# Seven products for eight in part of the input projection, with attention laid among the plain gate tiles

## The chip, the core and the metric

The kernel runs on one core of a Trainium2 chip. TensorE (PE) multiplies, VectorE (DVE) and ScalarE (ACT) work elementwise, GpSimd (POOL) and SyncE (SP) mostly issue transfers. The metric is the device time of one execution, in microseconds.

## The reference, cut to what matters

One layer of a streaming encoder on 1088 frames: 1024 of a new stream and 64 of a running one with a key and value cache.

```python
def mixer(xn, conv_prefix, attn_fn, w_in, w_conv, w_conv_out, w_attn_out, w_out):
    proj = xn @ w_in                      # 1024 -> 5120
    cb, cc, ch, q, k, v, ga, gb = jnp.split(proj, splits, axis=-1)   # 6 x 512, 2 x 1024
    cv, conv_state = causal_conv(cc * ch, conv_prefix, w_conv)
    ya = (cb * cv) @ w_conv_out
    o, new_k, new_v = attn_fn(heads(q), heads(k), heads(v))
    yb = o.reshape(B, L, ATT_DIM) @ w_attn_out
    merged = jax.nn.sigmoid(ga) * ya + jax.nn.sigmoid(gb) * yb
    return merged @ w_out, conv_state, new_k, new_v

x = x + mixer(rmsnorm(x, g_mix), ...)
x = x + swiglu(rmsnorm(x, g_ffn), w_ff1, w_ff3, w_ff2)      # 1024 -> 2816 -> 1024
return rmsnorm(x, g_final), ...           # and the rolled caches and convolution states
```

Attention has 8 heads of 64. Each chunk of 64 frames reads itself and the 8 chunks before it, with a bias by relative distance.

## The kernel before, in words

All matrix work is done in pairs of rounded numbers: `split` writes a high part (ScalarE, line 129) and the rest as a low part (VectorE, line 130), and a product is three matmuls, high by high, high by low and low by high (`product`, lines 182 to 184, weights of 128 columns stationary, frames moving).

The stages follow each other:

- **Head** (lines 354 to 455). For each of nine token tiles: `norm_tile` takes the sum of squares and the factor, transposes the tile on TensorE and copies it; `scale_tile` transposes the factor, scales by it and the gain, and splits into `xn`; `v_tile` makes the value columns (lines 423 to 425, 24 matmuls of 512 columns). `cache_tile` (line 456) turns the cached keys; keys, queries and values go to DRAM in the layout of heads.
- **Projection tiles**, 128 output columns each. `run_dense` makes one tile in three pieces of frames, `CH`: 384, 384 and 320, eight row blocks by three matmuls each, 72 matmuls. Order: q and k in turn (8 tiles), gate a (8), gate b (8). Gates go to DRAM (`ga_d`, `gb_d`).
- **Attention**, as a generator of 75 steps. A step makes the scores of one query tile (lines 570, 571), adds the bias (533), takes the exponential (543) and scales (545); it transposes an earlier step's tile (600) and splits it into `pt`; and it multiplies a still earlier one with the values (625) and adds halves (552 to 554). After each piece of the tiles from the fourth on, `between` runs `PER` = 1.16 steps. Scores and their transposes share the two buffers of `patt`.
- **Convolution**: 12 tiles cc, ch, cb by `dense` in the same pieces; in between, the attention output is read back from `o_d` and split into `ob` (line 757).
- **Merge**: `ya` and `yb`, 16 tiles of 36 matmuls, with the gates read back, sigmoid applied, and the sum split into `mg` (as quarters of 512 rows by 544 frames) and `ms`.
- **Output projection** (lines 843 to 848), norm and transposes (917), with `first_half` and `second_half` making the seven operands of the hidden layer (line 942 the differences).
- **Hidden layer**: `Unit` and `run` make two tiles at once in seven products of quarter matrices for eight (Strassen's way in Winograd's form): seven steps of 24 matmuls of 272 columns (line 1047), with sums of weights prepared a step at a time while the unit before runs, and results added from PSUM and snapshots.
- **Down projection** (line 1385), also by seven products, final norm and output.

The order of instructions on each engine is not simply that of the text. A planner with its own estimate of each instruction's duration goes through the program at compile time and gives each engine the first instruction, in text order, that it expects to be ready; pool buffers are handed out in the same pass. At run time each engine keeps the order it was given and waits on semaphores. SP and POOL issue the transfers, each in its own order.

Of the kernel before, what the change touches and what calls it, by code (L numbers as in the profile page):

```python
# [30 lines left out]
CH = [(0, 384), (384, 384), (768, 320)]  # L31
NC = len(CH)
# [6 lines left out]
AHEAD = 1  # L39
PER = 1.16  # L40


def spots(a, n):


    edges = [(0, 512, 0), (512, 1024, 544)]
    r = []
    for lo, hi, at in edges:
        s, e = max(a, lo), min(a + n, hi)
        if s < e:  # L50
            r.append((s - a, at + s - lo, e - s))
    return r


class Acts:


    def __init__(self, tiles):
        self.t = tiles

    def at(self, l, k, o, n):
        return self.t[k // 4][:, l, k % 4, o : o + n]

    def four(self, g, l, o, n):
        return self.t[g][:, l, :, o : o + n]


class Quarters:

# [4 lines left out]
    def at(self, l, k, o, n):  # L74
        h = o // HT
        return self.t[k // 4, h][:, l, k % 4, o - h * HT : o - h * HT + n]


@with_exitstack
def encoder_kernel(ctx: ExitStack, tc: tile.TileContext, ins, outs):  # L80
# [10 lines left out]
    a_stack = ExitStack()  # L91
    apool = a_stack.enter_context(tc.tile_pool(name="apool", bufs=1, reuse_waits="tile", side="right"))
    rpool = ctx.enter_context(tc.tile_pool(name="rpool", bufs=2, reuse_waits="tile"))
    w_stack = ExitStack()
    wpool = w_stack.enter_context(tc.tile_pool(name="wpool", bufs=3, reuse_waits="tile"))
# [7 lines left out]
    g_mix = cols[:, :KD]  # L103
# [4 lines left out]
    hs_d = dr.tile([NF // 2, P, 2, 2 * TS], F32, name="hs_d")  # L108
    q_d = dr.tile([NH, 2, HD, T], F32, name="q_d")
# [5 lines left out]
    bias_e = dr.tile([NH, 768], F32, name="bias_e")  # L115

    def bias_rows(h, a, n):
        return bias_e[h : h + 1, a : a + n].to_broadcast([P, n])
# [8 lines left out]
    def split(hi, lo, src, hi_eng=None):  # L127

        act.copy(hi, src)  # L129
        vec.tensor_tensor(lo, src, hi.bitcast(F32), op=ALU.subtract)  # L130

    def act_tiles(nm):
        return Acts([apool.tile([P, 2, 4, T], F32R, tag=f"A{g}", name=f"{nm}{g}") for g in range(2)])


    units = []
    loads = []

    def plan(view, kt, width, n):

        per = 1 if n == 1 else 2
        for i in range(0, n, per):
            ld = {"src": view[:, i * width : (i + per) * width], "kt": kt, "w": per * width}
            for j in range(per):
# [132 lines left out]
    def q_evac(hp):  # L277
# [7 lines left out]

        return f

    late = []

    def k_out(hp, k32, o, n):  # L290

# [1176 lines left out]
```

## Time and profile before

| | us |
|---|---|
| median of 3 runs (lowest, highest) | 1541.53 (1538.94, 1543.95) |
| the profiled execution | 1541.21 |
| its span, first to last instruction | 1539.3 |
| TensorE busy | 1500.1 |
| weight loads on TensorE busy | 1412.0 |
| VectorE busy | 928.0 |
| ScalarE busy | 623.4 |
| GpSimd busy | 77.5 |
| data moved | 247.18 MB, mean 161 GB/s |

The profile is of one execution. Shares are of the span. A matmul's record includes the time that it spends behind its neighbours, so matmul durations overlap; distances between starts show the rate. Names to the left of an arrow are written, names to the right are read.

### The profile page before, as it was taken

The page shows a single profiled execution, that of the slowest core. Times are in us where ns is not written, and L with a number is a line of the kernel's source. Part 1 is how long each engine was busy: PE and PEld are TensorE (multiplying, and loading weights), DVE is VectorE, ACT ScalarE, POOL GpSimd, SP SyncE. Part 2 cuts the span into 40 slices and gives each one's busy share as a digit, 9 for nine tenths or more (in the row PEclk, how much of TensorE's full clock was granted, in tenths as well). Part 3 has the DMA queues.
Part 4 walks back from the last instruction along what each step waited for, and adds up shares of the span by engine and source line. Part 5 has one row for each costly group of instructions (what it writes and reads, how often), then busy time and mean ns, then how long its engine had stood idle before and what let it go on. Part 6 is the DMA issues. An engine that isn't in the chain of part 4 may idle for free.

```text
span 1539.3 us, 24393 instructions
## 1 busy us (share of the span) xinstructions
PE 1500.1 (97%) x9407; PEld 1412.0 (92%) x9407; DVE 928.0 (60%) x1860; ACT 623.4 (40%) x1236; POOL 77.5 (5%) x146
## 2 busy tenths in 40 slices
PE   7999999999999999999998999999999999899997
PEld 6888999999999999998888999999999999688886
DVE  7524665555553434654379666666666667847677
ACT  7423454444443131543156444444444444502123
POOL 0110000000000000000000010000101111000000
PEclk9999999999999999999999999999999999999999
DMA  8688785444431323545432343333434438777685
GB/s 285 196 239 231 188 251 155 133 139 126 123 103 43 53 75 41 154 146 166 137 126 70 141 144 138 122 118 138 155 141 155 144 138 288 259 240 240 212 266 203
DMA packets 168661, 247.18 MB, mean 161 GB/s; under 512 B 17025, under 2 KB 117265, under 8 KB 168545
## 3 DMA queue, kind: packets, MB, share of 16 engines
q1 hardware_dynamic: 152400, 191.47, 41.1%
q0 software_dynamic: 14992, 52.05, 9.1%
q10 hardware_dynamic: 1152, 2.10, 0.4%
q8 instruction: 74, 1.21, 0.4%
q14 instruction: 43, 0.34, 0.1%
HBM read 161.91 MB, written 85.23 MB: 161 GB/s over the span
## 4 chain that ended last, share of the span: by engine, by line
PE 63%; issue 26%; DMA 4%; POOL 2%; DVE 2%; ACT 1%; SPq 1%; POOLq 0%; ACTq 0%; DVEq 0%
PE A L1385 7%; PE p L182 5%; PE p L183 5%; PE p L184 5%; PE D L1385 3%; PE B L1385 2%; POOL h_d L1105 2%; PE t L600 2%; PE pv L625 2%; PE Ab L1047 2%; DMA w2r<-in_w_ff 1%; PE Aa L1047 1%; PE ys L1242 1%; PE wo L843 1%; PE wo L844 1%
## 5 line engine op out<-in xcount | busy, mean ns | idle before, releaser
L182 PE MATMUL p<-xn,whi 128*128 128x384 f32 (+1 forms) x576 | 192.8, 335 | 0.1
L183 PE MATMUL p<-xn,whi 128*128 128x384 f32 (+1 forms) x576 | 189.2, 328 | 0.0
L184 PE MATMUL p<-xn,wlo 128*128 128x384 f32 (+1 forms) x576 | 189.0, 328 | 0.0
L1385 PE MATMUL A<-ring,ht 128*128 128x512 f32 x528 | 124.9, 390 | 3.9 <-ACT acc L1395 2.2
L1385 PEld LDWEIGHTS A<-ring,ht 128*128 128x128 f32 x528 | 98.7, 188 | 25.9 <-ACT acc L1395 3.5
L182 PEld LDWEIGHTS p<-xn,whi 128*128 128x128 f32 x576 | 109.2, 190 | 1.6 <-DVE kst L130 0.6
L183 PEld LDWEIGHTS p<-xn,whi 128*128 128x128 f32 x576 | 109.3, 190 | 0.1
L184 PEld LDWEIGHTS p<-xn,wlo 128*128 128x128 f32 x576 | 109.0, 189 | 0.0
L533 DVE CUSTOM_DVE_ANT_0 p<-s,bias 128x640 f32<-128x640 f32 (+5 forms) x72 | 47.7, 664 | 97.0 <-PE s L571 96.9
L129 ACT CAST ring<-w2r 128x512 fp32r<-128x512 f32 (+1 forms) x78 | 43.6, 588 | 103.6 <-PE A L1385 51.7
L129 ACT CAST hq<-sa 128x512 fp32r<-128x512 f32 x77 | 47.6, 619 | 89.5 <-DVE sa L1117 55.9
L129 ACT CAST whi<-raw 128x1024 fp32r<-128x1024 f32 x44 | 46.0, 1050 | 92.2 <-PE ch L183 42.5
L130 DVE TENSOR_TENSOR hq<-sa,hq 128x512 fp32r<-128x512 f32 x77 | 53.1, 689 | 37.5 <-ACT hq L129 37.4
L130 DVE TENSOR_TENSOR wlo<-raw,whi 128x1024 fp32r<-128x1024 f32 x44 | 53.7, 1220 | 24.0 <-ACT whi L129 23.9
L1047 PE MATMUL Aa<-tt,wha 128*128 128x272 f32 x352 | 60.9, 295 | 5.2 <-ACT tt L129 3.5
L1385 PE MATMUL D<-ring,ht 128*128 128x512 f32 x264 | 62.9, 390 | 1.4 <-ACT acc L1395 1.4
L130 DVE TENSOR_TENSOR wla<-rawa,wha 128x512 fp32r<-128x512 f32 x56 | 38.4, 687 | 42.3 <-ACT wha L129 42.3
L1105 POOL DMA_DIRECT2D h_d<-hq x77 | 41.0, 533 | 425.0 <-DVE hq L130 248.2
L1385 PEld LDWEIGHTS D<-ring,ht 128*128 128x128 f32 x264 | 49.5, 188 | 12.1 <-ACT acc L1395 1.8
L1047 PE MATMUL Ab<-tt,whb 128*128 128x272 f32 x352 | 58.9, 288 | 1.6 <-ACT whb L129 1.6
L1047 PE MATMUL Ab<-mg,whb 128*128 128x272 f32 x352 | 58.4, 288 | 0.0
L1047 PE MATMUL Aa<-mg,wha 128*128 128x272 f32 x352 | 58.3, 288 | 0.0
(310 smaller groups left out, 3888.1 us busy)
## 6 DMA issues: line engine op xcount, KB each, us to landing
h_d<-hq POOLq DMA_DIRECT2D x77, 512.0 KB, 3.5
ht<-h_d SPq DMA_DIRECT2D x154, 256.0 KB, 3.7
raw<-in_w_in SPq DMA_DIRECT2D x18, 1024.0 KB, 5.9
rawa<-in_w_ff SPq DMA_DIRECT2D x11, 1024.0 KB, 5.7
rawb<-in_w_ff SPq DMA_DIRECT2D x11, 1024.0 KB, 5.3
w2r<-in_w_ff SPq DMA_DIRECT2D x11, 1024.0 KB, 7.2
qd<-q_d SPq DMA_DIRECT2D x32, 272.0 KB, 4.4
x<-in_x_prompt SPq DMA_DIRECT2D x8, 512.0 KB, 4.2
```

What stands on the lines that cost most here:

```text
L129: act.copy(hi, src)
L130: vec.tensor_tensor(lo, src, hi.bitcast(F32), op=ALU.subtract)
L182: mm(out, a, p, start=k == 0, stop=False)
L183: mm(out, a, q, start=False, stop=False)
L184: mm(out, b, p, start=False, stop=k == kt - 1)
L533: vec.tensor_tensor_reduce(out=s if len(ps.shape) == 2 else s.rearrange("p (a b) -> p a b", a=2), in0=ps, in1=bias if len(ps.shape) == 2 e ...
L600: nc.tensor.transpose(tp[:, i * P : (i + 1) * P], s[:, i * P : (i + 1) * P], ident)
L625: mm(pv[:, :, lo:hi], v[:, kb, :], pt[:, :, kb - base, lo:hi], start=i == 0, stop=i == len(blocks) - 1,)
L843: mm(ps, x(k, 0), wh, start=f, stop=False)
L1047: mm(t[:, j, :HN], x[:, k, :], moving(p, l, k, j * HN, HN), start=p in (1, 2, 7) and k == 0 and n == 0, stop=k == 3 and n == 2, skip_group ...
L1105: nc.gpsimd.dma_start(h_d[p, c - 1], hq.rearrange("p i l t -> p (i l t)").bitcast(F32))
L1385: mm(t, ht[k][:, j, x], w[:, l], start=p in (1, 2, 7) and k == 0 and n == 0, stop=k == len(ks) - 1 and n == 2, skip_group_check=p in (6, 5 ...
```

## The change

The normed x is now made and kept as four quarters, like the input of the hidden layer, and the three sums that the seven products need (`xs6`, `xs7`, `xs5`) and a changed fourth quarter are formed in the head, tile by tile (`sums1`), in the order `ORDER` = 8, 0, 1, 4, 2, 5, 3, 6, 7. The scaling by factor and gain is done on rows ahead of the transposes. The plain fourth quarter goes to DRAM (`x21_d`).

Twelve units by seven products follow: q, k, the first four tiles of gate b, and the convolution's cc, ch and cb (two tiles a unit). Their results go to DRAM: q and k to heads, gate b, and the convolution's result `u_d`. The cache tiles are turned during the first two units. Then the plain quarter is read back, and twelve gate tiles (all of gate a, the other half of gate b) are made plainly in four pieces of 272 columns, with attention at `PER` = 2.25 steps a piece; attention ends ahead of the last two tiles (`LAST`), during which u and the attention output are read back. `ya` and `yb` are made in pieces of 272 too. One weight pool, `ws`, serves all stages. `Unit` and `run` are moved up and take operands, banks and snapshots as arguments. Frames are stored by halves of 544 (512 of the prompt, 32 of the sample).

The core of the diff:

```diff
-CH = [(0, 384), (384, 384), (768, 320)]
-NC = len(CH)
...
-AHEAD = 1
-PER = 1.16
...
+PER = 2.25
+LAST = 2
...
+    PIECES = [(j * HN, HN) for j in range(4)]
+    GATES = [("a", m) for m in range(8)] + [("b", m) for m in range(4, 8)]
...
-        for c in cs:
-            o, n = CH[c]
-            ps = pmm.tile([P, 512], F32, tag="mm", name=f"{nm}_{c}")
-            product(ps[:, :n], w, wsl, x, o, n, kt)
...
+    for k in range(KD):
+        nc.tensor.transpose(gp[:, k * P : (k + 1) * P], cols[:, k : k + 1].to_broadcast([P, P]), ident)
+    act.activation(gm, gp, AF.Copy, scale=-0.5)
...
+    def normed(i):
+        n = TT[i][1]
+        xt = xts[i]
+        a = FEW + 6 * (ORDER.index(i) % 2)
+        few = scr[:, a : a + 6]
+        act.activation(scr[:n, SQ : SQ + D], xt[:n], AF.Square, accum_out=few[:n, :1])
+        r = norm_factor(few[:, 1:], few[:n, :1], n, f"m{i}")
+        vec.scalar_tensor_tensor(xt[:n], xt[:n], r[:n], gm[:n], op0=ALU.mult, op1=ALU.mult)
...
+    def left_half(src, c, n):
+        for g in range(2):
+            both(xn.t[g, 0], c, n, src[:, g])
...
+        act.copy(f, src)
+
+    def right_half(src, c, n):
+        for g in range(2):
+            both(xn.t[g, 1], c, n, src[:, g])
+        nc.gpsimd.dma_start(
+            x21_d[:, :, c : c + n],
+            xn.t[0, 1][:, :, :, c : c + n].rearrange("p l k t -> p (l k) t").bitcast(F32),
+        )
...
+        minus(s[:, 0], src[:, 0], f[:, 0])
+        minus(s[:, 1], src[:, 1], s[:, 0])
+        both(t1[6], c, n, s[:, 1])
+        minus(f[:, 0], s[:, 1], f[:, 0])
+        both(t1[7], c, n, f[:, 0])
+        both(t1[5], c, n, s[:, 0])
+        minus(f[:, 1], f[:, 1], s[:, 1])
+        both(xn.t[0, 1], c, n, f[:, 1])
...
+    units = []
+    for nm, u in (
+        ("q", 0), ("q", 1), ("k", 0), ("k", 1), ("gb", 0), ("cc", 0), ("ch", 0), ("cb", 0), ("gb", 1), ("cc", 1),
+        ("ch", 1), ("cb", 1),
+    ):
...
+    turned1(ORDER[0])
+    for n, i in enumerate(ORDER):
+        if n + 1 < len(ORDER):
+            turned1(ORDER[n + 1])
+        if n + 3 < len(ORDER):
+            load_x(ORDER[n + 3])
+        if n + 2 < len(ORDER):
+            normed(ORDER[n + 2])
...
+        v_tile(i)
+        if n == len(ORDER) - 1:
+            for u in (u0, u1):
+                u.prep(0)
+                u.prep(1)
+        sums1(i)
...
+    def summed(src, snap):
+
+        if snap is None:
+            t = snap1(None, None)
+            whole(t, src, None)
+            return t
+        vec.tensor_tensor(snap, src, snap, op=ALU.add)
+        return snap.rearrange("p j n -> p (j n)")
...
+    def q_done(u):
+        def f(r, h, src, snap):
+            s = summed(src, snap)
+            st = stage()
+            act.activation(st[:, 0], s, AF.Copy, scale=0.125)
             vec.scalar_tensor_tensor(
-                st[:, 1, :n], ps, 0.125, st[:, 0, :n].bitcast(F32), op0=ALU.mult, op1=ALU.subtract
+                st[:, 1], s, 0.125, st[:, 0].bitcast(F32), op0=ALU.mult, op1=ALU.subtract
             )
-            to_heads(q_d, st, hp, o, n)
+            to_heads(q_d, st, 2 * u + r, h)
...
+    def k_done(u):
+        def f(r, h, src, snap):
+            kf = slot(CC, HT)
+            whole(kf, src, snap)
+            st = stage()
+            split(st[:, 0], st[:, 1], kf)
+            to_heads(k_d, st, 2 * u + r, h)
+            late.append(lambda: k_out(2 * u + r, h, kf))
...
+    def b_done(u):
+        def f(r, h, src, snap):
+            s = summed(src, snap)
+            nc.sync.dma_start(gb_d[(2 * u + r) * P : (2 * u + r + 1) * P, h * HT : (h + 1) * HT], s)
...
+    def cb_done(u):
+        def f(r, h, src, snap):
+            s = summed(src, snap)
+            for a, at, n in spans(h):
+                vec.tensor_tensor(s[:, a : a + n], s[:, a : a + n], ccs[r][:, at : at + n], op=ALU.mult)
+            st = stage()
+            split(st[:, 0], st[:, 1], s)
+            nc.sync.dma_start(u_d[2 * u + r, :, :, h * HT : (h + 1) * HT], st.bitcast(F32))
...
+    x7 = {p: xn.t[gh] for p, gh in PLAIN.items()} | t1
...
+        for _ in r:
+            if n < 2 and si in (2, 5):
+                i = 2 * n + si // 5
+                cache_tile(i)
+                if i + 2 < 4:
+                    cache_load(i + 2)
+            if si > 1:
+                for f in due:
+                    f()
+                due.clear()
+            due += late
             late.clear()
-            dense(xn, KD, tiles[i], w=w, cs=[c], nm=f"p{i}")
...
+            o, n = PIECES[c]
+            ps = pmm.tile([P, 512], F32, tag="mm", name=f"g{i}_{c}")
+            product(ps[:, :n], gate_w[i], xn, o, n)
+            st = st_pool.tile([P, HN], F32, tag="st", name=f"gst{i}_{c}")
+            act.copy(st[:, :n], ps[:, :n])
+            nc.sync.dma_start(dst[m * P : (m + 1) * P, o : o + n], st[:, :n])
...
-    run_dense(1)
     head_load(0)
+
+    nc.sync.dma_start(xn.t[0, 1].rearrange("p l k t -> p (l k) t").bitcast(F32), x21_d)
     bias_table(2)
-    for i in range(2, len(tiles)):
-        run_dense(i, between if i > 2 else None)
...
+    for i in range(2):
+        gate_w[i] = next_w()
+        gate(i, (0, 1))
+    for i in range(2):
+        for c in (2, 3):
+            gate(i, (c,))
+            if i:
+                between()
+    for i in range(2, len(GATES)):
+        gate_w[i] = next_w()
+        if i == len(GATES) - LAST:
+            for _ in steps:
+                pass
+            att_stack.close()
+            uo = pg_stack.enter_context(tc.tile_pool(name="uo", bufs=1, reuse_waits="tile"))
+            u = Acts(uo.tile([P, 2, 4, T], F32R, name="u"))
+            ob = Acts(uo.tile([P, 2, 4, T], F32R, name="ob"))
+            mp = pg_stack.enter_context(tc.tile_pool(name="mgp", bufs=5, reuse_waits="tile"))
+            for k in range(4):
+                nc.sync.dma_start(u.t[:, :, k].bitcast(F32), u_d[k])
+                t = mp.tile([P, T], F32, tag="ol", name=f"ol{k}", bufs=1)
+                nc.sync.dma_start(t, o_d[k * P : (k + 1) * P])
+                split(ob.t[:, 0, k], ob.t[:, 1, k], t)
+        for c in range(4):
+            gate(i, (c,))
+            between()
...
+    psum2 = pg_stack.enter_context(tc.tile_pool(name="psum2", bufs=5, space=PSUM, reuse_waits="tile"))
+    for m in range(8):
+        wa, wb = next_w(), next_w()
+        sg = {}
+        for o, n in PIECES:
+            for nm, src in (("ga", ga_d), ("gb", gb_d)):
+                t = sg[nm, o] = mp.tile([P, HN], F32, tag=nm, name=f"{nm}{m}_{o}")
+                nc.sync.dma_start(t, src[m * P : (m + 1) * P, o : o + n])
+                act.activation(t, t, AF.Sigmoid)
+            ya = psum2.tile([P, 512], F32, tag="mm", name=f"ya{m}_{o}")
+            product(ya[:, :n], wa, u, o, n)
+            vec.tensor_tensor(sg["ga", o], ya[:, :n], sg["ga", o], op=ALU.mult)
+        for o, n in PIECES:
+            t = sg["ga", o]
+            yb = psum2.tile([P, 512], F32, tag="mm", name=f"yb{m}_{o}")
...
```

More of the change, by code (lines that the diff above doesn't have):

```diff
@@ L271, in to_heads @@
+    def to_heads(dst, st, hp, h):
+        far = 0 if dst is q_d else CACHE
+        for row, at, m in ((512 * h, 0, 512), (TP + far + 32 * h, 512, 32)):
             for j in range(2):
@@ L1255, in up_run @@
         l, p = names[n]
-        return run(unit, (gate_done if l == "a" else hidden_done)(p), ahead)
+        return run(unit, operands, bank2, snap2, (gate_done if l == "a" else hidden_done)(p), ahead)
     u0, u1 = up_unit(0), up_unit(1)
```

970 lines of the change are left out of this document (436 added, 534 removed).

## The prediction

> **What bounds the kernel now.** I read the page first: its engine shares and its row of granted clocks.
>
> ```profile
> span 1539.3 us, 24393 instructions
> PE 1500.1 (97%) x9407; PEld 1412.0 (92%) x9407; DVE 928.0 (60%) x1860; ACT 623.4 (40%) x1236; POOL 77.5 (5%) x146
> PEclk9999999999999999999999999999999999999999
> ```
>
> TensorE is busy 97% of the span at full clock. VectorE has 40% to spare, ScalarE 60%. So columns taken off TensorE should show in the time, as long as the other engines and the transfers keep pace where the work is packed more tightly. Next came the table of busy time by stretch, for the stages that the change rebuilds (columns: stretch, its length, busy us and count for PE, PEld, DVE, ACT, POOL, then clock, DMA share, GB/s).
>
> ```profile
> 0.00:14.00 14.00, 5.82 (x24) 4.79 (x25) 5.90 (x19) 9.47 (x14) 1.39 (x7) 1.00 0.89 335
> 71.50:140.00 68.50, 60.92 (x354) 59.20 (x352) 20.00 (x48) 18.72 (x40) 8.58 (x15) 0.95 0.82 220
> 100.00:110.00 10.00, 6.20 (x29) 5.85 (x28) 4.43 (x8) 3.36 (x6) 2.02 (x3) 0.83 0.80 213
> 120.00:130.00 10.00, 7.39 (x48) 7.20 (x47) 0.81 (x6) 0.25 (x1) 0.00 (x0) 1.00 1.09 303
> 140.00:470.00 330.00, 328.94 (x2084) 319.27 (x2082) 191.27 (x475) 155.64 (x333) 5.28 (x8) 1.00 0.53 154
> 500.00:600.00 100.00, 100.00 (x607) 100.00 (x606) 42.87 (x66) 19.61 (x33) 0.00 (x0) 1.00 0.32 56
> ```
>
> From 140 to 470 us (q, k, gates with attention) and from 500 to 600 us (convolution) TensorE never rests. Between the value products and full attention, 71.5 to 140 us, it loses 7.6 us and some clock. The third view is TensorE in order of time, for its waits.
>
> ```profile
> 14.15 0.78 PE L423 MATMUL pvv<-wvh,xn 128*128 128x512 f32 x1
> 86.83 0.66 PE L456 MATMUL ckp<-ident,ct 128*128 128x128 f32 x4
> 105.11 0.90 PE L295 MATMUL ktp<-ident,k 128*128 128x128 f32 x3 [3.80 <-ACT k L318]
> 129.77 0.44 PE L570 MATMUL s<-kd,qd 128*128 128x384 f32 x1 [2.60 <-DVE mx L533]
> 712.56 0.80 PE L847 MATMUL wo<-woh,ms 128*128 128x512 f32 x1 [2.21 <-ACT woh L129]
> 831.85 0.39 PE L1047 MATMUL Ab<-tt,whb 128*128 128x272 f32 x1 [1.62 <-ACT whb L129]
> 836.92 0.82 PE L1047 MATMUL Aa<-tt,wha 128*128 128x272 f32 x2 [3.47 <-ACT tt L129]
> ```
>
> The four cache transposes at 86.83 run in the middle of the first q tile's products, though the program text has them after it: the order on an engine is the planner's, which puts ready work ahead of work it expects to be late.
>
> **What a column costs.** A busy matmul overlaps its neighbours, so I take distances between starts. Plain tiles go in pieces of 384, 384 and 320 columns, 72 products each. The 100 us from 500 to 600 hold 607 of them, 164.7 ns each, so a plain tile takes 72 x 0.1647 = 11.86 us. The seven-product form is already used for the hidden layer, and the chain of waits shows its steps of 24 products of 272 columns:
>
> ```profile
> 1223.58 3.01 PE Da L1047 x24
> 1226.59 3.01 PE Aa L1047 x24
> ```
>
> That is 125.4 ns a product. A unit of seven steps takes 21.07 us and yields two tiles, which cost 23.72 us plain.
>
> **The change, part by part.**
>
> (1) 24 tiles (four each of q, k and gate b, twelve of convolution) become twelve units: 24 x 11.86 = 284.6 us become 12 x 21.07 = 252.8. That is **-31.8 us** on TensorE, the bound.
>
> (2) The twelve other gate tiles and the sixteen ya/yb products go from three pieces to four of 272 columns. A gate tile has 96 products, 12.04 us: 12 x 0.18 = +2.2. A ya or yb has 48, 6.02 for 5.93: 16 x 0.09 = +1.4. **+3.6**.
>
> The Trainium skill ("TensorE: Matmul & The Clock Gate", section "Wait — 56ns, not 53.3ns?") gives a warm product columns / 2.4 GHz plus about 2.5 ns, which is 116 ns for 272 columns where this trace has 125. By that page part 1 would still be about -32 and part 2 an estimated +1.2 instead of +3.6; the measured pitch decides.
>
> (3) The head. The norm factor now scales whole rows, and nine small transposes of it go; eight transposes for the gain row come, and 24 key transposes for 20. About 0. The first value product waits for the gain row. Its columns come by the POOL queue in 5.6 us:
>
> ```profile
> cols<-in_cols POOLq DMA_DIRECT2D x1, 10.0 KB, 5.6
> ```
>
> With issue, eight transposes, a copy and a scaling I reach about 13 to 14 us, as now (14.15): **0**, ends -2 and +3. The seven operands cost VectorE eight more half-size instructions for each of four token tiles. The same work stands ahead of the hidden layer, and there
>
> ```profile
> 810.00:820.00 10.00, 10.00 (x61) 8.81 (x60) 9.81 (x18) 8.14 (x16) 0.54 (x1) 1.00 0.25 80
> 820.00:830.00 10.00, 9.99 (x81) 9.80 (x79) 10.00 (x20) 5.85 (x11) 0.54 (x1) 1.00 0.40 133
> 830.00:840.00 10.00, 4.89 (x25) 4.28 (x25) 10.00 (x18) 6.31 (x13) 0.00 (x0) 0.77 0.01 2
> ```
>
> VectorE is full while TensorE still runs, and then TensorE waits 1.62 + 3.47 us for the last sums and loses some clock. I take the same handover here: **+7**, ends 0 (the four opening steps, 12 us, hide it) and +12.
>
> (4) The cache tiles, the bias tables and the q, k stores now lie under units, and head 0 is fetched as the last unit drains. What TensorE lost between 71.5 and 140 goes: 7.6 idle and some 2.4 of slow clock (clock 0.83 from 100 to 110; 5% of the whole stretch, 3.4, bounds it). **-10**, ends -11 and -4. Stores with their SP issues run over four units, 84 us, so SP has room: q and k issue 64 of them, and issues like these take
>
> ```profile
> 123.27 5.43 SPq L272 DMA_DIRECT2D q_d<-qst  x6
> ```
>
> 0.9 us each at worst, 58 us.
>
> (5) One operand's place is reused for a sum, and the plain quarter (128 x 8 x 544 x 4 B = 2.2 MB) is read back once the last unit's sixth step is done, 3 us before the gates begin. At 303 GB/s (row 120 to 130) it takes 7.4 us, and head 0's 3.0 MB share the queue. It lands some 7 to 14 us into the gate stage. Cover: four half tiles that need no second half, 12 us. **+2**, ends 0 and +10.
>
> (6) Attention goes from 63 gate pieces at 1.16 steps to 34 at 2.25. TensorE from 140 to 470:
>
> ```profile
> 140.00:470.00 330.00, 156.17 (x471) 88.17 (x471) 1.00 0.53 154
> 140.00:470.00 330.00, 46.42 (x136) 1.00 0.53 154
> ```
>
> (first line the products of line 182, second the score additions of line 533, two records a step.) 471 x 3 x 0.1647 = 232.7 us of tiles leave 97 us for 68 steps, 1.43 each. After, a step gets 34 x 3.01 / 72 + 1.43 = 2.85 us of TensorE. VectorE spent 191 us here, less some 32 for weights (the first row below, from 117 to 478 us) and q, k stores, 2.34 a step, plus 0.2 for gate weights: 2.5 of 2.85. It fits, at 89%.
>
> ```profile
> L130 DVE TENSOR_TENSOR wlo<-raw,whi 128x1024 fp32r<-128x1024 f32 x22 | 26.8, 1219 | 2.3 <-ACT whi L129 2.3
> L533 DVE CUSTOM_DVE_ANT_0 p<-s,bias 128x640 f32<-128x640 f32 x32 | 26.2, 820 | 40.5 <-PE s L571 40.5
> L544 DVE RECIPROCAL rc<-sm 128x1 f32<-128x1 f32 x64 | 10.2, 159 | 8.4 <-ACT p L543 7.4
> L545 DVE TENSOR_SCALAR p<-p,rc 128x640 f32<-128x640 f32 x32 | 17.6, 548 | 0.7
> L130 DVE TENSOR_TENSOR pt<-t,pt 128x640 fp32r<-128x640 f32 x32 | 26.2, 820 | 8.3 <-ACT pt L129 7.7
> ```
>
> Against it speak the waits among three engines, for it the rows 810 to 830, where VectorE ran full and TensorE still was. **+2**, ends 0 and +15.
>
> (7) Two gate tiles and the first ya (24.1 + 6.0 = 30 us) cover the reload of u (4 x 1.11 MB) and the attention output (4 x 0.56 MB), which goes through one buffer.
>
> ```profile
> L129 ACT CAST ob<-ol x12: 458/512/517, 545.5 to 567.3; 128x384 fp32r<-128x384 f32 x8, 128x320 fp32r<-128x320 f32 x4
> L130 DVE TENSOR_TENSOR ob<-ol,ob x12: 484/555/559, 546.8 to 567.8; 128x384 fp32r<-128x384 f32 x8, 128x320 fp32r<-128x320 f32 x4
> DMA to landing us min/median/max: 2.3/2.4/3.3
> ```
>
> 6.7 MB at 303 GB/s are 22 us. Each of four rounds also has a landing of 2.4 and, scaled to 1088 columns, a cast of 1.4 and a subtraction of 1.5, in part beside the next u. I get 27 to 35 us: **+5**, ends 0 and +22 (below).
>
> The skill's page "DMA: Bandwidth & Descriptors" (Specifications) puts the limit of HBM for one core at about 358 GB/s; by that estimate the bytes take 19 us and this term is 0. This trace's best stretch shows 335.
>
> (8) The weight pool no longer changes hands ahead of the output projection, where 2.21 us were lost: **-1**, ends -2 and 0.
>
> Sum: -31.8 + 3.6 + 0 + 7 - 10 + 2 + 2 + 5 - 1 = -23.2. The profiled execution took 1541.2 us (span 1539.3 and 1.9 around it), 0.3 below the median of the three runs, 1541.5. So **1518 us**.
>
> **The rivals.**
>
> (A) Attention becomes the bound: slower. Place: gate tiles 1 to 9. Scores and their transposes share two PSUM buffers; a full step has an addition (0.82), the exponential, a reciprocal (0.16), a scaling (0.55), five transposes, a cast and a subtraction (0.82) in sequence, with the other engines' parts some 5 us, and VectorE at 89% can make each wait for the last. It decides from 3.25 us a step: 72 x 0.4 = 29 us, all of the gain. At 3.5 it costs 47 us: 1565 - 2 already counted, about **1563**. For it: the density doubles. Against: VectorE's short instructions overlap by about 0.08 us when queued (0.68 long at 0.60 distance below), so its 2.5 us shrink.
>
> ```profile
> 811.61 0.68 DVE L130 TENSOR_TENSOR mg<-xt,mg 128x512 fp32r<-128x512 f32 x1
> 812.21 0.68 DVE L861 TENSOR_TENSOR x<-wo,x 128x512 f32<-128x512 f32 x1
> ```
>
> (B) The reload (7) blocks the gates. If the four casts stand ahead of the gate copies on ScalarE, three PSUM buffers hold 9 us of products and TensorE waits until the last load lands at 27 to 31: 18 to 22 us, 15 more than counted: **1534**, still just faster. Against: the twelve casts of before are spread over 22 us, and TensorE was full there (row 500 to 600).
>
> (C) The handovers (3) and (5) both cost their upper ends: 5 + 8 more, **1531**.
>
> (D) Everything is hidden: (3), (5), (6), (7) near 0: **1502**.
>
> (E) It doesn't bring what it says: 2016 products replace 1728, and if a product's fixed cost were larger the seventh saved would vanish. The two pitches above exclude it.
>
> **How the numbers follow.** Forecast case (1510 to 1526) 0.47; D 0.13; C 0.13; B 0.13; A 0.14, spread from 1536 up. A difference under 0.3%, 4.6 us, is about what a measurement of this kernel can't tell from none. Faster than 1536.9: forecast, D, C and most of B, 0.78. Within: the rest of B and the mild part of A, 0.10. Slower than 1546.1: 0.12. The range of 8 in 10 is 1501 to 1537: it leaves out A's larger part and little else. The likeliest case alone has 1510 to 1526.
>
> **What would show it.** Right: twelve units at 21.1 us each with TensorE without a gap (1); no wait like those at 105 and 130 (4); steps of 2.9 us in attention (6). Wrong: an idle stretch of TensorE of over 8 us at the last value tile, at the first gate tile that needs the second half, or ahead of the first yb; VectorE over 95% busy while TensorE has gaps in attention; or units longer than 22 us because VectorE can't finish q's, the convolution's and the next weights' work in 21.

## The result, and the profile after

| | before | after |
|---|---|---|
| median, us (lowest, highest; four runs each) | 1540.88 (1538.94, 1543.95) | 1566.94 (1561.12, 1568.55) |
| profiled execution, its span | 1541.21, 1539.3 | 1561.12, 1559.3 |
| TensorE busy, idle (span less busy) | 1500.1, 39.2 | 1481.3, 78.0 |

The change made the kernel 26 us slower: ratio 1.016, 95% interval 1.0129 to 1.0192. The forecast was 1518, range 1501 to 1537. One execution of a run below, f1, took 2418 us at a granted clock of 0.56 and is left out of its figures. The page of the changed kernel is of the fastest of its four executions, whose span grew by 20.0 us; the other three took 5 to 7 us more. It shows both halves of the change. TensorE does have less to do, but it rests twice as long:

```profile
span 1559.3 us, 26380 instructions
PE 1481.3 (95%) x10178; PEld 1387.8 (89%) x10178; DVE 1008.3 (65%) x1989; ACT 681.7 (44%) x1382; POOL 70.5 (5%) x133
PE   5699999997999999999998999999999999899998
PEclk9899999998999999999999999999999999999999
```

In the row of slices TensorE falls short at the start and in the tenth slice (351 to 390 us). The table by stretch, in the columns of the prediction's fences, and then TensorE in order of time:

```profile
40.00:80.00 40.00, 25.63 (x115) 20.72 (x115) 26.23 (x55) 21.95 (x43) 6.02 (x10) 0.83 0.54 161
200.00:300.00 100.00, 100.00 (x801) 99.98 (x800) 60.50 (x100) 37.39 (x64) 0.00 (x0) 1.00 0.48 126
357.00:400.00 43.00, 32.70 (x222) 31.62 (x223) 10.87 (x27) 9.52 (x20) 0.00 (x0) 0.84 0.90 272
400.00:580.00 180.00, 169.93 (x1234) 158.69 (x1233) 140.37 (x398) 112.39 (x260) 0.00 (x0) 1.00 0.58 159
```

```profile
18.02 1.11 PE L398 MATMUL xt<-ident,scr 64*128 64x64 f32 x8 [10.30 <-DVE scr L384]
...
47.20 3.82 PE L398 MATMUL xt<-ident,scr 128*128 128x128 f32 x16 [7.21 <-DVE scr L384]
...
74.86 1.94 PE L398 MATMUL xt<-ident,scr 128*128 128x128 f32 x8 [6.18 <-DVE scr L153]
...
357.05 0.77 PE L234 MATMUL Dcb<-xn,whcb 128*128 128x272 f32 x4 [3.23 <-ACT scr L222]
...
384.52 0.46 PE L836 MATMUL s<-kd,qd 128*128 128x128 f32 x2 [2.88 <-DMA qd<-q_d]
387.26 0.77 PE L837 MATMUL s<-kd,qd 128*128 128x128 f32 x2 [2.27 <-DMA qd<-q_d]
391.98 0.69 PE L836 MATMUL s<-kd,qd 128*128 128x384 f32 x1 [3.95 <-DVE mx L794]
...
463.00 0.66 PE L866 MATMUL t<-ident,p 128*128 128x128 f32 x4 [1.81 <-DVE pt L118]
...
516.74 0.66 PE L866 MATMUL t<-ident,p 128*128 128x128 f32 x4 [2.18 <-DVE pt L118]
...
647.61 0.52 PE L292 MATMUL yb<-ob,whp 128*128 128x272 f32 x2 [0.41 <-ACT ob L117]
...
853.71 0.39 PE L234 MATMUL Ab<-tt,whb 128*128 128x272 f32 x1 [1.62 <-ACT whb L117]
...
858.79 0.82 PE L234 MATMUL Aa<-tt,wha 128*128 128x272 f32 x2 [3.47 <-ACT tt L117]
```

The units run with 3.4 us idle from 100 to 340 us. The time is lost in three places: the head (a start 6.8 us later, then 14 us idle from 40 to 80 us, and a clock of 0.83), the handover from the units to gates and attention (10 us idle from 357 to 400, clock 0.84), and, once for each of the last six heads, attention (10 us from 400 to 580). The wait at 357.05 stands apart: it is still in the last unit. The last two rows are those of before at 831.85 and 836.92, 22 us later and with the same waits; at the end of the span 20.0 us are left. Starts of some first products, with the best version found below (e5) beside them:

| us | before | after | e5 |
|---|---|---|---|
| first, last value product | 14.15, 70.91 | 20.90, 96.85 | 19.89, 79.28 |
| first gate piece; first score | | 365.83; 384.52 | 347.48; 368.91 |
| first output projection | 712.56 | 734.77 | 697.17 |

### The profile page after: what moved, and what is told of

Same layout as the page of the kernel before. It is cut to its first block, busy times and chain, and to the rows that moved or that the text cites. A ratio compares the mean times of both kernels' runs of the same rounds, so it can differ in the third digit from the quotient of the medians.

```text
span 1559.3 us, 26380 instructions
## 1 busy us (share of the span) xinstructions
PE 1481.3 (95%) x10178; PEld 1387.8 (89%) x10178; DVE 1008.3 (65%) x1989; ACT 681.7 (44%) x1382; POOL 70.5 (5%) x133
## 4 chain that ended last, share of the span: by engine, by line
issue 73%; PE 17%; POOL 3%; DMA 3%; DVE 2%; ACT 1%; SPq 0%; POOLq 0%; ACTq 0%
PE A L1447 7%; PE D L1447 3%; POOL h_d L1168 2%; PE B L1447 2%; PE Ab L234 1%; DMA w2r<-in_w_ff 1%; PE Aa L234 1%; PE ys L1305 1%; DMA wv<-in_w_in 1%; PE Db L234 1%; PE Da L234 1%; DMA h_d<-hq 0%; PE Bb L234 0%; POOL x_d L1057 0%; POOL x_d L1070 0%
## 5 line engine op out<-in xcount | busy, mean ns | idle before, releaser
L292 PE MATMUL g<-xn,whp 128*128 128x272 f32 x384 | 113.5, 296 | 1.1 <-ACT scr L525 1.0
L294 PE MATMUL g<-xn,wlp 128*128 128x272 f32 x384 | 112.4, 293 | 0.0
L293 PE MATMUL g<-xn,whp 128*128 128x272 f32 x384 | 112.3, 293 | 0.0
L292 PEld LDWEIGHTS g<-xn,whp 128*128 128x128 f32 x384 | 73.0, 190 | 2.0 <-ACT scr L525 1.2
L293 PEld LDWEIGHTS g<-xn,whp 128*128 128x128 f32 x384 | 73.1, 190 | 0.7
L294 PEld LDWEIGHTS g<-xn,wlp 128*128 128x128 f32 x384 | 72.9, 190 | 0.1
L804 ACT ACTIVATE p<-p,mx 128x640 f32<-128x640 f32 (+5 forms) x72 | 50.9, 707 | 20.2 <-DVE mx L794 19.2
L117 ACT CAST wha<-rawa 128x512 fp32r<-128x512 f32 x56 | 34.8, 622 | 53.6 <-PE Ab L234 36.6
L118 DVE TENSOR_TENSOR ring<-w2r,ring 128x512 fp32r<-128x512 f32 (+1 forms) x78 | 48.9, 646 | 14.3 <-ACT ring L117 14.1
```

Of the source, the lines that this page charges most:

```text
L292: mm(out, a, p, start=k == 0, stop=False)
L293: mm(out, a, q, start=False, stop=False)
L294: mm(out, b, p, start=False, stop=k == kt - 1)
L804: act.activation(s, s, AF.Exp, bias=mx, scale=-1.0, accum_out=sm)
```

## The experiments

**The theories.** Q: ScalarE, VectorE and SP each stand, in their fixed order, at an instruction that waits for a transfer, and work that TensorE needs is queued behind it. Rivals: V, the arithmetic of the seven operands is too much for VectorE and ScalarE in the head; B, the bytes of the handover set its length; A, attention at 2.25 steps a piece is too dense. Under Q, places (slots of scratch memory in which data waits for its transfer) and queues can be changed with arithmetic and bytes as they are, and the time falls. Times are medians; ratios are to the kernel before, whose median in these comparisons was 1541.4 to 1542.0. Gains and losses in us are counted from the 1566.9 of the table above, or from the run that is named.

### The head

ScalarE and GpSimd in order of time, changed kernel:

```profile
30.92 0.56 POOL L467 DMA_DIRECT2D out_cache_v_sample<-scr  x1 [3.56 <-ACT scr L462]
...
40.31 0.58 ACT L117 CAST scr<-pvv 128x512 fp32r<-128x512 f32 x1 [5.22 <-DMA v_d<-scr]
...
42.76 1.06 ACT L382 ACTIVATE scr<-scr 128x1024 f32<-128x1024 f32 x1
...
43.94 1.06 ACT L382 ACTIVATE scr<-scr 128x1024 f32<-128x1024 f32 x1
...
45.12 1.06 ACT L382 ACTIVATE scr<-scr 128x1024 f32<-128x1024 f32 x1
...
77.64 1.06 ACT L382 ACTIVATE scr<-scr 128x1024 f32<-128x1024 f32 x1 [3.50 <-DMA out_cache_v_prompt<-scr]
```

Three squares (line 382), the first step of the norm of three token tiles, run at 42.8 to 46.1, though their x had been asked for at 19, 21 and 29. TensorE has run out of transposed x by then. Two waits stand ahead of them: a value cast for the one place `VST` of the value store, and the place `SQ`, which squares share with plain value rows (`v32`) on their way to the cache output.

**e1: both places told apart.**

```diff
-        put_v(scr[:, VST : VST + D], pv, n, t0 if t0 < TP else TP + CACHE)
+        o = ORDER.index(i)
+        if o < 7:
+            st = t1[(6, 5)[o % 2]][:, :, :, 384:512].rearrange("p l k (e d) -> p (l k) e d", e=2)
+        else:
+            a = (GM, KEPT[0])[o - 7]
+            st = scr[:, a : a + D]
+        put_v(st, pv, n, t0 if t0 < TP else TP + CACHE)
...
-            v32 = scr[:, SQ : SQ + ATT]
+            a = VST + ATT * (o % 2)
+            v32 = scr[:, a : a + ATT]
```

> The changed kernel, with places in the head told apart: the pair of a value tile that waits for its store gets two places (columns of two of the seven-product operands that are written last) for one, and the plain value rows for the cache output no longer share a place with the squares. Instructions and transfers are the same. Theory Q (queues held by a store): in the changed kernel ScalarE stood 5.2 and 5.1 us ahead of a value cast for a store out of the one place, and 3.5 us ahead of a square for the cache output, with the norm of the next tokens behind it, and the x loads followed those on SP. Then TensorE's 30.6 us idle and 2.7 us of slow clock between 0 and 100 us shrink to 10 to 15, and the time falls by 15 to 22 us from 1567, to 1545 to 1552. Rival V (the work of the seven operands on VectorE and ScalarE is what is late, however it is queued): the waits move to other instructions and the gain is under 5 us. Rival D (the early transfers, 250 us GB/s and more, are late whatever waits for them): under 5 us too, with x loads landing as late.

1551.0 us, ratio 1.005 (1.0033 to 1.0067): 16 us of the loss gone, as Q had it. The arithmetic is the same, so V falls as the cause of these 16 us.

**g1 and g2: one half each.** g1 writes the squares, whose values nobody reads, as bf16 in half the place, and `v32` in the other half. g2 gives the value store two places and leaves `SQ` shared.

```diff
-        act.activation(scr[:n, SQ : SQ + D], xt[:n], AF.Square, accum_out=few[:n, :1])
+        act.activation(
+            scr[:n, SQ : SQ + ATT].bitcast(mybir.dt.bfloat16), xt[:n], AF.Square, accum_out=few[:n, :1]
+        )
...
-            v32 = scr[:, SQ : SQ + ATT]
+            v32 = scr[:, SQ + ATT : SQ + D]
```

> Half of the first edit. The changed kernel, with the squares (of which only the sum is used) written as bf16 into one half of their place and the plain value rows for the cache output into the other, so that the two no longer wait for each other; the pair for the value store still has one place. Theory S: the shared place is the cause. A square must wait there for the store of value rows, so the planner puts the squares of the next three tiles behind two later value casts, and they run at 42.8 to 46.1, when TensorE has run out at 40. Apart, they run as in the run with both edits: 1548 to 1555. Theory W (the one place for the pair of the value store, as the profile's wait of 5.2 us names it): the wait stays, 1562 to 1568.

> The other half of the first edit. The changed kernel with two places for one for the pair of the value store; squares and plain value rows still share one. Theory S: ScalarE's order stays that of the changed kernel, squares behind two value casts, and the time too: 1562 to 1568. Theory W: 1548 to 1555.

g1: 1549.1, ratio 1.0044 (1.0029 to 1.0059), all of e1's gain. g2: 1558.2, ratio 1.0105 (1.0089 to 1.0121), about half. ScalarE in order of time, g1 first:

```profile
32.73 1.06 ACT L382 ACTIVATE scr<-scr 128x1024 bf16<-128x1024 f32 x1 [1.71 <-DMA scr<-in_x_prompt]
...
38.35 1.06 ACT L382 ACTIVATE scr<-scr 128x1024 bf16<-128x1024 f32 x1 [0.57 <-DMA scr<-in_x_prompt]
```

```profile
38.98 0.59 ACT L117 CAST xs<-pvv 128x512 fp32r<-128x512 f32 x1 [5.02 <-PE pvv L459]
...
41.43 1.06 ACT L383 ACTIVATE scr<-scr 128x1024 f32<-128x1024 f32 x1
```

In g1 the squares run as x lands. In g2 the value cast no longer waits for a store, but 5.0 us for its product, and the squares still stand behind it: ScalarE's order there is that of the changed kernel. So the shared place cost twice. A square waits in it for a store (3.5 us at 77.64 in the changed kernel); and the planner puts the squares behind two value casts as long as the place is shared, which I take for its foreseeing that wait. I had expected g2 to give nothing, and it gave 9 us; the wait for the value store was real too, but once the squares run in time, the second value place of e1 brings nothing beyond g1.

### The handover and attention

ScalarE, SP and VectorE, changed kernel:

```profile
355.87 0.62 ACT L117 CAST whp<-rawp 128x512 fp32r<-128x512 f32 x1 [6.54 <-DMA rawp<-in_w_in]
...
361.88 0.34 SPq L927 DMA_DIRECT2D xn<-x_d  x1
362.31 3.63 SPq L654 DMA_DIRECT2D u_d<-scr  x2
...
374.36 0.65 ACT L117 CAST scr<-scr 128x544 fp32r<-128x544 f32 x1 [8.58 <-DMA u_d<-scr]
...
375.79 0.51 SPq L654 DMA_DIRECT2D u_d<-scr  x1
376.36 0.60 SPq L765 DMA_DIRECT2D kd<-k_d  x1
...
391.07 0.11 DVE L784 MEMSET bias<- 64x64 f32 x1 [15.31 <-DMA bias<-in_bias_ext]
391.81 0.39 ACT L756 COPY gst<-g 128x272 f32<-128x272 f32 x1 [16.24 <-DMA ga_d<-gst]
```

The first row is behind TensorE's wait at 357.05: a cast waits for weights to land, and the copy that TensorE needs follows it. This is a wait of the same kind, and no run below is aimed at it. The reload of the plain quarter (2.2 MB) leaves just ahead of a store of u. The last cast of u waits 8.6 us for that store's place, SP waits for the cast, and head 0's transfers start only at 376.4. Then a gate piece's copy waits 16.2 us for a gate store that stands behind them on SP, and TensorE has no PSUM buffer left to write a gate product to. VectorE in turn stands 15.3 us at a fill of head 0's bias tile, with the score addition behind it that TensorE waits for at 391.98. The Trainium skill's page "PSUM — Partial Sum Buffer" (section "Engine vs sequencer instructions") calls the queues of ScalarE, VectorE and GpSimd strictly first in, first out; the rows of ScalarE and VectorE here agree.

**e2: four places for u in the last unit**, **e3: the corner fills of the bias tile on GpSimd**, **f3: gate stores issued by GpSimd**, each alone.

```diff
-            st = stage()
+            if u == 1 and h == 1:
+                st = scr[:, UT[r] : UT[r] + 2 * HT].bitcast(F32R).rearrange("p (l n) -> p l n", l=2)
+            else:
+                st = stage()
...
-        vec.memset(b[HD:, :HD], NEG)
-        vec.memset(b[:HD, 576:], NEG)
+        pool_e.memset(b[HD:, :HD], NEG)
+        pool_e.memset(b[:HD, 576:], NEG)
...
-            nc.sync.dma_start(dst[m * P : (m + 1) * P, o : o + n], st[:, :n])
+            nc.gpsimd.dma_start(dst[m * P : (m + 1) * P, o : o + n], st[:, :n])
```

> The changed kernel, with four places for two for the pairs of u that the last unit stores (the two that the convolution has left). Theory Q: ScalarE stood 8.6 us (365.8 to 374.4) ahead of the last cast for a store that had 2.2 MB of the plain quarter's reload ahead of it, SP stood behind that cast, and head 0's transfers started at 376.4; with the places they start near 367, the first scores near 376 instead of 384.5, and 6 to 10 us of the 13.5 us idle and 4.2 us of slow clock between 340 and 400 go: 1557 to 1561. Rival B (bytes: reload, head 0, weights and u are some 7.4 MB, 27 us at the 272 GB/s of that stretch): the first scores come as late, the gain is under 3 us.

> The changed kernel, with the two fills of the bias tile's corners on GpSimd for VectorE. Theory Q: once a head VectorE stands up to 2.4 us at these fills for the bias transfer, with the subtraction behind it that frees the buffer of the next transposes; these are the 10.1 us that TensorE waits for pt, in seven waits. They go, and the time falls by 7 to 10 us, to 1557 to 1560. Rival A (attention at 2.25 steps a piece is too dense for VectorE and the two buffers): the waits turn up at other instructions, the gain is under 3 us.

> The changed kernel with the gate stores issued by GpSimd, and nothing else. Theory Q: ScalarE's 16.2 us (375.6 to 391.8) ahead of a gate copy go, but the last u cast still waits 8.6 us and head 0 starts at 376; 4 to 9 us less, 1558 to 1563. If the two edits need each other: under 3 us, 1564 or more.

e2: 1560.9, ratio 1.0136 (1.0119 to 1.0153), 6 us less; its interval overlaps that of the changed kernel, so this run alone does not show the gain (h3 below does). e3: 1552.1, ratio 1.006 (1.0041 to 1.0079), 15 us, more than the 7 to 10 expected. f3: 1549.4, ratio 1.0046 (1.0028 to 1.0063), 18 us, twice what I expected. Why attention waits once a head, and why f3 mends that too, stands in SP and VectorE, changed kernel first, then f3:

```profile
457.75 0.58 SPq L780 DMA_DIRECT2D bias<-in_bias_ext  x1
458.43 0.38 SPq L781 DMA_DIRECT2D bias<-bias_d  x1
...
461.86 0.11 DVE L784 MEMSET bias<- 64x64 f32 x1 [1.71 <-DMA bias<-in_bias_ext]
462.43 0.11 DVE L785 MEMSET bias<- 64x64 f32 x1 [0.45 <-DMA bias<-bias_d]
```

```profile
443.23 0.58 SPq L780 DMA_DIRECT2D bias<-in_bias_ext  x1
...
447.66 0.52 SPq L781 DMA_DIRECT2D bias<-bias_d  x1
448.04 0.11 DVE L784 MEMSET bias<- 64x64 f32 x1
```

The two fills wait on VectorE for the bias, the last transfer of the next head; the subtraction that frees a PSUM buffer for the next transposes is right behind them (TensorE's wait at 463.00). With the gate stores gone from SP the first part of the bias is issued earlier in its head, ahead of `v`, and the first fill finds it landed; the second fill then comes 3.3 us later, by itself. In both e3 and f3 TensorE's idle time between 400 and 600 us fell from 10.1 to 0.2 us or less (e3 first):

```profile
400.00:600.00 200.00, 199.80 (x1460) 187.91 (x1459) 166.42 (x453) 133.55 (x308) 3.30 (x14) 1.00 0.54 151
400.00:600.00 200.00, 199.98 (x1462) 188.10 (x1461) 166.79 (x465) 132.34 (x306) 17.27 (x32) 1.00 0.54 150
```

The Trainium skill's page "DMA: Bandwidth & Descriptors" (section "Issuing engines are not separate DMA queues") says that starting transfers from several engines saves only the issue time, usually a small thing. No run here speaks against its shared transfer engines, but the 18 us of f3 are of another kind: what SP holds back while it waits, not what an issue takes. From `kd` to the first bias transfer of the head above, SP took 16.0 us in the changed kernel, of which the issues of two gate stores are 0.9, and 8.6 in f3. Here the measurement decides.

**h3: the full set (e5, below) with two places for u again.**

> The run with gate stores on GpSimd (1523.2), with two places again for u in the last unit. Theory Q: the cast waits again some 8 us for a u store behind the reload, head 0 starts 8 to 10 us later on SP, and 3 to 8 us come back: 1526 to 1531. If gate stores were the whole handover: 1521 to 1525.

1531.3, ratio 0.9931 (0.9917 to 0.9944), 8 us above e5, with intervals apart: both remedies of the handover are needed.

### Together

**e4** = e1 + e2 + e3. **e5** = e4 + f3. **h1** = g1 + e2 + e3 + f3, with one place for the value store.

> The changed kernel with the three edits of the other runs together. Theory Q: the gains lie in separate stretches and add: 28 to 42 us, 1525 to 1539, faster than the kernel before. Rivals V, B and A together: under 11 us, 1556 or more.

> The version with all three edits, and the stores of the gate tiles issued by GpSimd for SP. Theory Q: there ScalarE stood 20.4 us (355 to 375.4) ahead of the third copy of a gate piece, since its place waited for a store that SP had queued behind head 0's thirteen transfers, and TensorE idled 10.4 us and ran at 0.57 to 0.92 of its clock. On their own queue the stores leave at once, four or more gate pieces run while head 0 lands, and 8 to 12 us go: 1522 to 1526 from 1534. Rival B (the bytes): reload, u, weights and head 0 take 27 to 30 us of transfers whatever the queue, the gate pieces run earlier but TensorE waits for the second half or the first scores all the same; under 3 us.

> The changed kernel with four small edits: squares as bf16 in one half of their place, four places for u in the last unit, fills of the bias tile on GpSimd, gate stores issued by GpSimd. Theory Q: the first edit alone gave 18 us where two places for the value store gave 9, so this set does what the set with gate stores did (1523.2): 1520 to 1526.

e4: 1534.2, ratio 0.9951 (0.9939 to 0.9963). ScalarE in e4, in order of time, still shows the handover, a gate copy that waits for a store behind head 0:

```profile
375.37 0.39 ACT L767 COPY gst<-g 128x272 f32<-128x272 f32 x1 [20.45 <-DMA ga_d<-gst]
```

e5: 1523.2, ratio 0.9885 (0.9872 to 0.9898), 44 us below the changed kernel and 18 below the one before. h1: 1528.4, ratio 0.9918 (0.9904 to 0.9931); I had expected it to equal e5. In its trace it is 0.5 us behind e5 at the last value product, 2.7 at the first gate piece and 4.7 at the first score, so most of its 5 us arise behind the head. Whether the one value place or another order brings them, these runs do not tell. e5 by stretch:

```profile
0.00:100.00 100.00, 82.80 (x456) 69.74 (x457) 76.94 (x153) 61.56 (x120) 13.84 (x27) 1.00 0.75 232
340.00:400.00 60.00, 55.20 (x419) 52.88 (x418) 30.17 (x77) 26.95 (x59) 6.84 (x15) 1.00 0.94 276
400.00:560.00 160.00, 160.00 (x1164) 150.30 (x1164) 135.26 (x376) 108.18 (x254) 16.06 (x38) 1.00 0.57 157
```

In attention TensorE is full while VectorE is busy 85% (135.26 of 160): A falls at this density. The handover now moves 276 GB/s at a share of 0.94 with 4.8 us idle; what is left of it may be bytes.

### What did not help further

**e6**: first halves of three gate tiles ahead, attention in 32 pieces at 2.36 steps. **f2**: three places for gate pieces. **e7**: e4 with the cache copies and bias tables out of the first 20 us and the gain's columns first on SP. **e8**: e4 with the gain's columns first on SP alone. **f1**: e5 + e7's edits + f2's. **h2**: e5 + e7's edits, bias tables spread only under later units.

> As the run with gate stores on GpSimd, and the first halves of three gate tiles for two ahead of everything else, with attention in 32 pieces at 2.36 steps for 34 at 2.25. Both remedies for the handover together: 9 to 14 us less than with the three edits alone, 1520 to 1525. Under rival A (attention's density) VectorE at 2.5 us of work in a step of 2.70 us makes waits of some 5 to 15 us between 380 and 580: 1530 or more, slower than the run with 2.25.

> The run with gate stores on GpSimd, with three places for two for the gate pieces on their way to DRAM. There ScalarE still stood 18.6 us between 350 and 382 for gate stores that landed some 6 us after their issue. Theory Q: 1 to 4 of the 4.8 us idle in the handover go, 1519 to 1522. Rival B (bytes): head 0 and the reload set the pace, 1522 to 1524.

> The version with all three edits, with the early transfers that nobody needs early taken out of the first 20 us: the cache outputs go from the rows that the cache tiles load, as in the kernel before, for copies from DRAM to DRAM; the bias tables are spread after the head, from a copy of the bias as in the kernel before; and the gain's columns come first on SP for POOL. Theory D for the start (1.8 MB of copies and 0.4 MB of tables delay the value weights, which land at 13.9 to 15.2 where the kernel before had all at 11.6): the first value product comes at 15 to 17 for 21.2, and 4 to 6 us go, to 1528 to 1530. Theory O (the order alone, gain copy behind weight casts): the same as the run with the gain's columns on SP alone.

> The version with all three edits, with the gain's columns loaded first on SP for POOL; the planner then puts the gain's copy ahead of the last four weight casts for ahead of three. Theory O: ScalarE's order costs the start, the first value product comes at 17 to 19 and 2 to 4 us go. Theory D: the copy still stands behind two casts that wait for their weights, under 1 us.

> The run with gate stores on GpSimd, plus the early transfers moved out of the first 20 us, plus three places for two for gate pieces on their way to DRAM. The earlier run on the early transfers brought the first value product from 21.2 to 16.3 but gave it back at 95 to 100 us and in the handover (a cast of a cache tile stood 7.7 us for a store; gate stores were still on SP). With the handover open, 3 to 8 us should stay: 1515 to 1520 against 1523. Rival: the cache tile's cast and the byte-bound handover take it again, 1521 to 1524.

> The run with gate stores on GpSimd, with the early transfers out of the first 20 us as before, but the bias tables now spread under the seventh-product units of gate b and the convolution (from about 180 us) for 86 us, where they stood ahead of a value store that held ScalarE for 7.7 us. Theory D: the first value product at 16 to 17 and no new wait; 4 to 6 of the 5 us stay: 1517 to 1520. Theory N (the start costs nothing, since the next tokens' x, norm and sums set the pace of the head anyway): 1521 to 1524.

| | us | ratio (interval) | beside |
|---|---|---|---|
| e6 | 1528.3 | 0.992 (0.9907, 0.9932) | e5 1523.2 |
| f2 | 1523.2 | 0.9882 (0.9868, 0.9896) | e5 1523.2 |
| e7 | 1533.8 | 0.995 (0.9938, 0.9962) | e4 1534.2 |
| e8 | 1539.6 | 0.9987 (0.9974, 0.9999) | e4 1534.2 |
| f1 | 1521.8 | 0.9867 (0.9852, 0.9881) | e5 1523.2 |
| h2 | 1523.4 | 0.9892 (0.9875, 0.9908) | e5 1523.2 |

None gave the gain that was hoped for. f2, f1 and h2 came out where their rivals had them: for f2 that is the bytes, while h2's rival had no gain at the start, and its trace shows one. e6 is not slower by density: TensorE was busy 159.0 of 160 us from 400 to 560. It lost 6.6 us at one transpose in the handover, where an exponential stood behind a gate copy that waited 6.9 us for its store. e7 shows a gain given back. Its first value product started at 16.3 instead of 21.2, and then ScalarE and TensorE, in order of time, show

```profile
99.11 0.62 ACT L119 CAST scr<-scr 128x512 fp32r<-128x512 f32 x1 [7.66 <-DMA v_d<-scr]
...
100.29 1.27 PE L236 MATMUL Dq<-xn,whq 128*128 128x272 f32 x4 [4.65 <-ACT scr L224]
```

a cast of a cache tile behind a store, with the bias tables (moved there by this edit) issued just ahead. In h2 they are moved further, and that wait is gone, but another stands at their new place:

```profile
188.91 4.18 POOL L115 DMA_DIRECT2D bias_d<-bias_e  x8 [72.56 <-DMA bias_e<-scr]
190.87 0.44 SPq L176 DMA_DIRECT2D rawch<-in_w_in  x1
...
202.61 1.14 ACT L119 CAST whch<-rawch 128x512 fp32r<-128x512 f32 x2 [9.01 <-DMA rawch<-in_w_in]
```

A cast waits 9.0 us for weights that were asked for just behind the tables, and TensorE 2.45 us (at 204.3) for the copy behind that cast. Beside e5, h2 is ahead by 6.5 us at the last value product (72.76 for 79.28), 3.9 at the first gate piece, 2.0 at the first output projection, and not at all at the end. So the start's 5 us can be won, but the rest of the schedule gives them back, in several waits. e8's 5 us of loss is larger than the edit explains: its trace is 1.0 us ahead of e4's at the last value product and 5.2 behind at the first gate piece, so the loss arises in the units. What made it is open.

## Why the prediction was wrong, point by point

The profiled execution (1561) lies 43 us above the forecast (1518). Of these, 19 were there at the last value product, which came 26 us later than before where step (3) had +7. Another 26 arose from there to the first output projection: that stretch took 641.7 us before and 637.9 after, where steps (1), (2) and (4) to (8) had 30.2 less. Some 2 us came back behind it.

- **(1), (2) products: right.** 801 products in the 100 us from 200 on are 124.8 ns each, 20.97 us a unit for 21.07. With the waits mended (e5) TensorE's busy time is 1474.4 us, 25.7 below before; steps 1 and 2 had 28.2. (In the changed kernel it is only 18.8 below, with stretches of slow clock in it.) The estimate of 116 ns for 272 columns, from the Trainium skill's page "TensorE: Matmul & The Clock Gate" (section "Wait — 56ns, not 53.3ns?"), was not seen.
- **(3) the head: wrong, the largest error.** It took the first value product at 13 to 14 us, with +3 as the worst; it came at 20.9. The gain's rows were ready for ScalarE near 8 us, but their copy ran at 15.6, behind weight casts that had waited 3.7 and 1.0 us for their weights. With other transfers out of the first 20 us (e7) the first value product came at 16.3 instead of 21.2; with the gain's columns first alone (e8), at 20.7. It then had +7 for a handover to the units that did not show at all: the first q product starts at 97.1, right behind the last value product. In between the step counted VectorE's instructions and not the places: nine value tiles, nine squares and five plain copies through single places, each held by a store. The last value product came 26 us later than before; 16 to 18 us of time came back in e1 and g1. In e5 it is still 8.4 us later. That this is near the +7 is luck: 5.7 of it is the start, which the step had at 0.
- **(4) the loss ahead of attention: right for the units only.** From 100 to 340 us 3.4 us are idle, where before it was 8.6 with slow clock beside it. But the wait of before at 129.77, for the first scores, did not go: it came back in the handover, 9.1 us in three waits. And "SP has room", 58 of 84 us, was the wrong question: a queue with room still stops at one wait.
- **(5) the reload: wrong.** +2 with an end of +10. From 340 to 400 us 13.5 us were idle, and the clock was 0.89; 3.2 of them are the wait at 357.05. The reload itself, which the step feared, held no gate piece. The step costed when the bytes land; it did not ask what the same queue would hold: the u store behind the reload, head 0 behind the u cast, the gate stores behind head 0. With these apart (e5) 4.8 us remain, within the step's range.
- **(6) attention: the mechanism was wrong, the size inside its ends.** 10.1 us for +2. The forecast share of VectorE, 89%, was near (85% with TensorE full, e5). The loss was two fills of 0.11 us that waited for a transfer. The same fills had waited in the kernel before:

```profile
128.84 0.11 DVE L523 MEMSET bias<- 64x64 f32 x1 [11.72 <-DMA bias<-bias_e]
...
194.88 0.11 DVE L523 MEMSET bias<- 64x64 f32 x1 [1.00 <-DMA bias<-bias_e]
```

  The first stood ahead of TensorE's 2.60 us at 129.77, a row of the prediction; later ones cost next to nothing at the old density (from 140 to 470 us TensorE was busy 328.94 of 330). Rival A named the right stage, but for the wrong reason.
- **(7) the late reload: +5 was too much.** TensorE waited 0.41 us at a yb product (647.61). The estimate from the Trainium skill's page "DMA: Bandwidth & Descriptors" (Specifications), 0, was nearer, but by luck: it had the bytes take 19 us, and from the first load (617.7) to the end of the last subtraction (648.9) it was 31, within the step's 27 to 35. What was better than forecast is the cover: TensorE had gate pieces and first yb products to do. Rival B did not occur.
- **(8): right.** The 2.21 us are gone; another wait, of 1.01 us, comes 10 us into the output projection.

The forecast was 1518, and with the waits mended the kernel takes 1523: the terms for work held, the terms for handovers did not. What was weighed there was whether each engine and queue had enough time, not who stands behind whom. The prediction's own list of what would show it wrong (idle over 8 us at the first gates) came near one of the three places, the 9.1 us at the first scores among the first gate pieces; for the head it looked only at the last value tile, and for attention at VectorE above 95%.

## What to carry to other kernels

Before costing a denser schedule, list every place (a slot of scratch, a staging buffer) that a transfer must empty before it is written again, and for each ask what stands behind the writer on its engine. A share of busy time, of an engine or of a queue, says nothing on that: ScalarE was busy 44%, and by step (4) SP had 84 us for 58 us of issues. Such waits are cheap to mend (half a scratch place, two fills on an idle engine, one store on another queue), and here they were worth more than the arithmetic saved. A planner may also put work later because of a shared place, as the squares here, so a place can cost time even where the profile shows no wait on it.

## What the runs showed that I had not expected

- The stores of one line on another queue, with the same bytes, were worth 17.6 us (f3), in two stages at once.
- The edits of single places did not add: 15.9, 6.0, 14.8 and 17.6 us alone are 54, together (e5) 43.7. e3 and f3 both mend the 10 us of attention, which the sum counts twice.
- Short idle stretches of TensorE cost more than their length. After the 7.2 us wait ahead of 47.2 the granted clock was 0.50 from 45 to 50 us and 0.92 from 50 to 55; after the three waits of 384 to 392 the gate products start every 0.227 us until 395, for 0.126 in the first gate pieces.
- What was won at the start (h2, 6.5 us at the last value product) was gone by the end, with no single wait to account for it.
